# Gate/up products of the FFN by seven block products in place of eight, and SwiGLU values split at the down projection

## The chip, the core and the metric

The kernel runs on one core of one Trainium2 chip. The metric is the device time of one execution in microseconds (us), as the median of several executions. The engines are TensorE (PE, with its weight loads as PEld), VectorE (DVE), ScalarE (ACT), GpSimd (POOL) and SyncE (SP, which here only issues transfers). Each engine works through its own instructions in their order. A matmul sums into a bank of PSUM; VectorE and ScalarE read PSUM, GpSimd works on SBUF here.

## What is computed

One transformer block on 512 latent tokens and 256 context tokens of width 1024: adaLN, a token mixer of retention and latent attention, an output projection, and then the part that the change touches, two norms around a SwiGLU FFN with D_FF = 2816:

```python
def _swiglu(h, w_gu, w_down):
    a, b = jnp.split(h @ w_gu, 2, axis=-1)
    return (jax.nn.silu(a) * b) @ w_down
...
        x = _layer_norm(alpha * x + g1 * y_l, ln1_g[i], ln1_b[i])
        x = _layer_norm(alpha * x + g2 * _swiglu(x * (1.0 + s2) + sh2, w_gu[i], w_down[i]), ln2_g[i], ln2_b[i])
```

All operands are float32. `w_gu` is 1024 x 5632: `a` (gate) and `b` (up) have 2816 columns each, that is 22 column tiles of 128.

## The kernel before

**Pairs.** [...] `split` (L104) makes a pair: ScalarE copies the operand with rounding to H (L105), VectorE subtracts H from it and has L (L106). `mm3` multiplies two pairs by three matmuls, HH (L121), HL (L122) and LH (L123). `weight` loads 512 KB of a weight from SyncE's queue and splits it.

**Stages around the change.** The tokens are two halves (`tp`) of 256. The output projection ends with a half's `first_norm`, which makes the normalised rows `z` and then, in `to_features`, transposes them on TensorE (L863), applies the modulation and splits the result to `h2`, the moving operand of gate/up: 8 k-blocks of 128 features by 512 tokens. While the second half is normalised, the first half of NEARLY = 2 early column tiles runs (matmuls of 256 columns, weights `wgh`, `wgl`); their second half follows.

Then come the other 20 column tiles, one after the other. Each has two weights, gate and up, and for each of them 8 k-blocks x 3 matmuls of 512 columns into a bank `gu` of its own: 48 matmuls. `activate` reads both banks: ScalarE's silu of the gate (L916), VectorE's multiply with the up product (L917), and a split into the pair `tt` for the down projection (L105, L106).

The down projection has 22 weights. Its first pass (`pair_mm`) does the first two tiles of 128 tokens with each weight, 12 matmuls of 512 columns; the second pass does the other two, with the last norm of the first ones beside it, and ends in `last_norm`, whose additions on POOL (L1019) are among the last operations. The rows `z` of the first norm stay in SBUF as `x1`; they are scaled by `ln1_g` and `ln1_b` in the middle of the gate/up stage and used as the residual.

**What sets the order.** The code is written in the order wanted, and a tile layer turns it into one instruction stream per engine, with semaphores for what must wait. Buffers come from pools: three raw weights, three pairs of weights, pages of 4 KB per partition, 8 buffers `e8` and 6 `hp`, two PSUM buffers of two banks (`big`) and four of one bank (`bank`). A tile can be written again when all that read it are done; this is kept per tile, not per part of it.

## Time and profile before

| | |
|---|---|
| median of 3 runs | 1004.62 us (1004.43 to 1005.13) |
| span of the profiled execution | 1001.1 us |
| time of the median around that span | 3.5 us |
| instructions in the trace | 11924 |
| TensorE busy | 97% of the span, 4652 matmuls |
| VectorE, ScalarE, GpSimd busy | 62%, 40%, 4% |

The profile is of one execution. The span runs from its first to its last instruction. The device time has some microseconds around it; here the median of the runs is 3.5 us above this span. "L123" is line 123 of the kernel; matmuls are pipelined, so one begins while the one before it is still shown as busy.

### The profile page before, as it was taken

What the parts mean: (1) busy time and instruction counts of PE and PEld (TensorE: products, weight loads), DVE (VectorE), ACT (ScalarE), POOL (GpSimd) and SP (SyncE); (2) the same over time, 40 slices, a digit from 0 to 9 for tenths busy, and PEclk for the clock granted to TensorE, in tenths of its full rate; (3) what the DMA queues carried; (4) which work ended last, traced back from release to release, by engine and by line L of the source; (5) the groups of instructions that cost most, each with busy time, mean ns of one, the idle gap of its engine ahead of it and who ended that gap; (6) DMA issues with size and microseconds to landing.
All of it is one profiled execution on the core that took longest, in us unless ns stands there. A gap on an engine that the chain in (4) does not pass through costs nothing.

```text
span 1001.1 us, 11924 instructions
## 1 busy us (share of the span) xinstructions
PE 971.0 (97%) x4652; PEld 790.0 (79%) x4652; DVE 616.5 (62%) x945; ACT 400.2 (40%) x596; POOL 42.2 (4%) x77
## 2 busy tenths in 40 slices
...
GB/s 356 317 137 200 238 78 44 22 64 48 28 96 156 136 211 255 152 79 22 0 1 64 150 206 150 84 84 90 100 126 105 87 102 89 148 208 190 213 229 60
DMA packets 40360, 128.22 MB, mean 128 GB/s; under 512 B 6768, under 2 KB 7920, under 8 KB 40304
## 3 DMA queue, kind: packets, MB, share of 16 engines
...
q0 software_dynamic: 640, 1.57, 0.8%
q8 instruction: 36, 0.59, 0.2%
q14 instruction: 20, 0.16, 0.1%
...
## 4 chain that ended last, share of the span: by engine, by line
PE 90%; DVE 5%; DMA 2%; ACT 1%; POOL 1%; issue 1%; POOLq 0%; SPq 0%; DVEq 0%; ACTq 0%
PE gu L122 8%; PE gu L123 8%; PE gu L121 8%; PE wd L122 4%; PE wd L121 4%; PE wd L123 4%; PE gt L121 3%; PE gt L123 3%; PE gt L122 3%; PE rva L121 1%; PE rva L123 1%; PE rva L122 1%; PE st L121 1%; PE av L121 1%; PE po L654 1%; PE po L656 1%
## 5 line engine op out<-in xcount | busy, mean ns | idle before, releaser
L106 DVE TENSOR_TENSOR w<-wr,w 128x1024 fp32r<-128x1024 f32 (+2 forms) x158 | 190.0, 1204 | 186.1 <-ACT w L105 185.7
L105 ACT CAST w<-wr 128x1024 fp32r<-128x1024 f32 (+2 forms) x158 | 163.1, 1033 | 268.3 <-issue 78.8
L123 PE MATMUL gu<-h,w 128*128 128x512 f32 x320 | 126.6, 396 | 0.0
L122 PE MATMUL gu<-h,w 128*128 128x512 f32 x320 | 126.5, 395 | 0.0
L121 PE MATMUL gu<-h,w 128*128 128x512 f32 x320 | 125.9, 393 | 0.0
L122 PEld LDWEIGHTS gu<-h,w 128*128 128x128 f32 x320 | 60.2, 188 | 14.6
L121 PEld LDWEIGHTS gu<-h,w 128*128 128x128 f32 x320 | 60.0, 188 | 14.4
L123 PEld LDWEIGHTS gu<-h,w 128*128 128x128 f32 x320 | 60.1, 188 | 13.7
L122 PE MATMUL wd<-w,tt 128*128 128x512 f32 (+1 forms) x163 | 61.0, 374 | 0.0
L123 PE MATMUL wd<-w,tt 128*128 128x512 f32 (+1 forms) x163 | 60.9, 374 | 0.0
L121 PE MATMUL wd<-w,tt 128*128 128x512 f32 (+1 forms) x163 | 60.7, 373 | 0.0
L121 PE MATMUL gt<-hL,w 128*128 128x512 f32 x128 | 50.9, 398 | 0.2 <-DVE ck L484 0.2
L122 PE MATMUL gt<-hL,w 128*128 128x512 f32 x128 | 50.7, 396 | 0.0
L123 PE MATMUL gt<-hL,w 128*128 128x512 f32 x128 | 50.7, 396 | 0.0
L917 DVE TENSOR_TENSOR sa<-gu,sa 128x512 f32<-128x512 f32 (+1 forms) x24 | 15.5, 646 | 56.9 <-PE gu L123 55.7
L916 ACT ACTIVATE sa<-gu 128x512 f32<-128x512 f32 (+1 forms) x24 | 13.5, 564 | 83.4 <-PE gu L123 83.4
L149 DVE SCALAR_TENSOR_TENSOR junk<-wr,sc 128x1024 bf16<-128x1024 f32 x20 | 24.5, 1223 | 26.6 <-DMA wr<-in_wada_dram 25.9
L121 PEld LDWEIGHTS wd<-w,tt 128*128 128x128 f32 x163 | 30.6, 188 | 6.1
L123 PEld LDWEIGHTS wd<-w,tt 128*128 128x128 f32 x163 | 30.7, 188 | 6.0
L122 PEld LDWEIGHTS wd<-w,tt 128*128 128x128 f32 x163 | 30.6, 188 | 6.0
L405 POOL TENSOR_SCALAR sm<-sm 128x1 f32<-128x1 f32 x18 | 7.8, 436 | 639.0 <-DVE sm L825 562.6
L106 DVE TENSOR_TENSOR pt<-ex,pt 128x512 fp32r<-128x512 f32 x48 | 30.7, 686 | 4.0 <-ACT pt L105 4.0
...
## 6 DMA issues: line engine op xcount, KB each, us to landing
wr<-in_w_gu_dram SPq DMA_DIRECT2D x44, 512.0 KB, 3.5
wr<-in_w_dn_dram SPq DMA_DIRECT2D x44, 512.0 KB, 3.5
wr<-in_wada_dram SPq DMA_DIRECT2D x20, 512.0 KB, 4.1
wr<-in_w_out_dram SPq DMA_DIRECT2D x16, 512.0 KB, 3.4
ada_m<-in_wada_dram SPq DMA_DIRECT2D x12, 512.0 KB, 6.2
ada_s<-in_wada_dram SPq DMA_DIRECT2D x8, 512.0 KB, 8.9
ada_h<-in_wada_dram SPq DMA_DIRECT2D x8, 512.0 KB, 8.9
wr<-in_w_rg_dram SPq DMA_DIRECT2D x8, 512.0 KB, 8.9
```

The lines of the kernel that those rows point to most:

```text
L105: S.copy(h, src)
L106: V.tensor_tensor(l, src, h.bitcast(F32), ALU.subtract)
L121: T.matmul(o, st[0], mv[0], start=start, stop=False)
L122: T.matmul(o, st[0], mv[1], start=False, stop=False)
L123: T.matmul(o, st[1], mv[0], start=False, stop=stop)
L149: V.scalar_tensor_tensor(junk, raw, 1.0, vec, ALU.mult, ALU.mult, accum_out=acc[:, b:b + 1])
L405: G.tensor_scalar(dst, src, scale, eps, ALU.mult, ALU.add)
L654: T.matmul(po[:65], vh, pt[:, 0], start=j == 0, stop=False)
L656: T.matmul(po[:65], vh, pt[:, 1], start=False, stop=j == NTA - 1)
L916: S.activation(sa, pab[0], AF.Silu)
L917: V.tensor_tensor(sa, pab[1], sa, ALU.mult)
```

## The change

A column tile's gate and up weights together are a matrix of 1024 x 256, seen as 2 x 2 blocks of 512 x 128: A11, A12 are the gate's two halves of k, A21, A22 the up's. The moving operand is 2 x 2 blocks of 512 features by 256 tokens: B11, B12 the first 512 features of the two halves of tokens, B21, B22 the other 512. The change forms the product of the blocks by the seven products of Winograd's form of Strassen's scheme, for 20 tiles. The first two tiles keep eight.

- Weights: S1 = A21 + A22, S2 = S1 - A11 on VectorE (L986, L987), S3 = A11 - A21, S4 = A12 - S2 on POOL (L988, L989), each 128 x 512 per tile, and then six pairs per two tiles in place of four: the gate's whole weight, S1 with S2, S3 with S4 (128 x 1024 each), and A22 (128 x 512).
- Moving operand, once: T1 = B12 - B11, T2 = B22 - T1 on VectorE, T3 = B22 - B12, T4 = B21 - T2 on POOL, each 128 x 1024 and split.
- Products, each 4 k-blocks x 3 matmuls of 256 columns: P1 = A11 B11, P2 = A12 B21, P3 = S4 B22, P4 = A22 T4, P5 = S1 T1, P6 = S2 T2, P7 = S3 T3. A tile has 84 such matmuls. The sums of products are in part made in PSUM: P6, P7 and P4 accumulate on P1 in the bank `gy`, P3 on P5 in `gz`; P2 has a bank `gx`. Between them ScalarE copies the sum after P1 (L1016), P6 (L1026) and P5, and VectorE reads it after P2 (L1021), P7 (L1035), P3 (L1039) and P4 (L1044).
- Tiles come in ten pairs; each product runs for both tiles of a pair in turn, and the two `gy` banks are one tile of the pool (`big("gy")`). The weights' loads, sums and splits of the next pair are written between the products.
- The SwiGLU values stay float32 in pages `tv`, and `hidden` splits them at the down projection, one tile per weight of the first pass.
- `to_features` makes the features of four k-blocks in one page `hx` and splits them in twos (`hb`); the rows `z` go to DRAM (`zkeep`), from ScalarE's queue, and come back (`kept`) in the first pass of the down projection.

The diff, cut to its core:

```diff
+    def pair_pages(src, n):
+        a, b = page([P, 4, 256], F32R, n + "h"), page([P, 4, 256], F32R, n + "l")
+        for j in range(0, 4, 2):
+            split(a[:, j:j + 2], b[:, j:j + 2], src[:, j:j + 2])
+        return a, b
     def to_features(tp, zs):
-        c = slice(tp * 256, tp * 256 + 256)
         for g in range(2):
             ps = big("zt")
             for f in range(4):
                 for i in range(2):
                     T.transpose(ps[:, f // 2, (f % 2) * 256 + i * P:(f % 2) * 256 + (i + 1) * P],
                                 zs[i][:, (4 * g + f) * P:(4 * g + f + 1) * P], ident)
-            for f in range(4 * g, 4 * g + 4):
-                src = ps[:, f % 4 // 2, (f % 2) * 256:(f % 2 + 1) * 256]
-                S.activation(h2[f][:, 0, c], src, AF.Identity, bias=sh2[:, f:f + 1], scale=sc2[:, f:f + 1])
-                hf = half([P, 256], n="hf")
-                if f % 2 == 0:
-                    V.tensor_scalar(hf, src, sc2[:, f:f + 1], sh2[:, f:f + 1], ALU.mult, ALU.add)
+            hf = hx[g, tp] = page([P, 4, 256], n="hx")
+            for j in (0, 2, 1, 3):
+                f = 4 * g + j
+                src = ps[:, j // 2, (j % 2) * 256:(j % 2 + 1) * 256]
+                if j < 2:
+                    V.tensor_scalar(hf[:, j], src, sc2[:, f:f + 1], sh2[:, f:f + 1], ALU.mult, ALU.add)
                 else:
-                    S.activation(hf, src, AF.Identity, bias=sh2[:, f:f + 1], scale=sc2[:, f:f + 1])
-                V.tensor_tensor(h2[f][:, 1, c], hf, h2[f][:, 0, c].bitcast(F32), ALU.subtract)
+                    S.activation(hf[:, j], src, AF.Identity, bias=sh2[:, f:f + 1], scale=sc2[:, f:f + 1])
+            hb[g, tp] = pair_pages(hf, "hb")
             yield
...
+            nc.scalar.dma_start(zkeep[2 * tp + i], z)
...
-                feat_mm(ps[:, :256], wg[2 * f + s], lambda k: (h2[k][:, 0, c], h2[k][:, 1, c]))
+                feat_mm(ps[:, :256], wg[2 * f + s], lambda k: (hb[k // 4, tp][0][:, k % 4], hb[k // 4, tp][1][:, k % 4]))
                 pab.append(ps[:, :256])
-            activate(pab, tt[f], c, 256)
-    x1 = zs[0] + zs[1]
-    for f in range(NEARLY, FT):
-        pab = []
-        for s in range(2):
-            w = weight(w_gu[2 * f + s])
-            ps = bank("gu")
-            feat_mm(ps, feat(w), lambda k: (h2[k][:, 0], h2[k][:, 1]))
-            pab.append(ps)
-        t = (eight if f < 8 else page)([P, 2, NL], F32R, "tt")
-        activate(pab, t, slice(0, NL), NL)
-        tt.append(t)
-        if f == 9:
-            l1g = rowb(lnrow[0])
-            l1b = rowb(lnrow[1])
-        if 9 <= f < 13:
-            V.tensor_tensor(x1[f - 9], x1[f - 9], l1g, ALU.mult)
-            V.tensor_tensor(x1[f - 9], x1[f - 9], l1b, ALU.add)
+            sa = half([P, 256], n="sa")
+            S.activation(sa, pab[0], AF.Silu)
+            V.tensor_tensor(tv[0][:, f, c], pab[1], sa, ALU.mult)
+    def moving(src, n):
+        a, b = eight([P, 4, 256], F32R, n + "h"), eight([P, 4, 256], F32R, n + "l")
+        split(a, b, src)
+        return a, b
+    def difference(a, b, n, eng):
+        t = page([P, 4, 256], n=n)
+        eng.tensor_tensor(t, a, b, ALU.subtract)
+        return t
+    t1 = difference(hx[0, 1], hx[0, 0], "t1", V)
+    t2 = difference(hx[1, 1], t1, "t2", V)
+    T2 = moving(t2, "t2")
+    T1 = moving(t1, "t1")
+    t3 = difference(hx[1, 1], hx[0, 1], "t3", G)
+    T3 = moving(t3, "t3")
+    t4 = difference(hx[1, 0], t2, "t4", G)
+    T4 = moving(t4, "t4")
+    B11, B21, B22 = hb[0, 0], hb[1, 0], hb[1, 1]
+    def product(o, st, mv, more=False):
+        for k in range(4):
+            c = slice(k * P, (k + 1) * P)
+            mm3(o, (st[0][:, c], st[1][:, c]), (mv[0][:, k], mv[1][:, k]), k == 0 and not more, k == 3, more)
+    class Hidden:
+        def __init__(self, f):
+            self.f = f
+        def loads(self):
+            self.a = load(w_gu[2 * self.f], 1024)
+            self.b = page([P, 1024], n="wgb")
+            nc.sync.dma_start(self.b, w_gu[2 * self.f + 1])
+        def sums(self):
+            ga, gb = self.a, self.b
+            s = self.s12 = page([P, 2, 512], n="s12")
+            d = self.s34 = page([P, 2, 512], n="s34")
+            V.tensor_tensor(s[:, 0], gb[:, :512], gb[:, 512:], ALU.add)
+            V.tensor_tensor(s[:, 1], s[:, 0], ga[:, :512], ALU.subtract)
+            G.tensor_tensor(d[:, 0], ga[:, :512], gb[:, :512], ALU.subtract)
+            G.tensor_tensor(d[:, 1], ga[:, 512:], s[:, 1], ALU.subtract)
+        def split_a(self):
+            w = whl.tile([P, 2, 1024], F32R, tag="w", name=nm("w"))
+            split(w[:, 0], w[:, 1], self.a)
+            self.a11, self.a12 = [(w[:, 0, c], w[:, 1, c]) for c in (slice(0, 512), slice(512, 1024))]
+        def halves(self, s, n):
+            a, b = page([P, 2, 512], F32R, n + "h"), page([P, 2, 512], F32R, n + "l")
+            split(a, b, s)
+            return [(a[:, i], b[:, i]) for i in range(2)]
+        def split_12(self):
+            self.s1, self.s2 = self.halves(self.s12, "s12")
+        def split_34(self):
+            self.s3, self.s4 = self.halves(self.s34, "s34")
+        def split_22(self):
+            w = page([P, 2, 512], F32R, "a22")
+            split(w[:, 0], w[:, 1], self.b[:, 512:])
+            self.a22 = w[:, 0], w[:, 1]
+        def p1(self):
+            self.o = tv[self.f // 2][:, self.f % 2]
+            self.qz = half([P, 2, 256], n="qz")
+            product(self.y, self.a11, B11)
+            S.copy(self.qz[:, 0], self.y)
+        def p2(self):
+            x = bank("gx")[:, :256]
+            product(x, self.a12, B21)
+            V.tensor_tensor(self.o[:, :256], x, self.qz[:, 0], ALU.add)
+        def p6(self):
+            self.ub = half([P, 2, 256], n="ub")
+            product(self.y, self.s2, T2, True)
+            S.copy(self.ub[:, 0], self.y)
+        def p5(self):
+            self.z = bank("gz")[:, :256]
+            product(self.z, self.s1, T1)
+            S.copy(self.qz[:, 1], self.z)
+        def p7(self):
+            product(self.y, self.s3, T3, True)
+            V.tensor_tensor(self.ub[:, 1], self.y, self.qz[:, 1], ALU.add)
+        def p3(self):
+            product(self.z, self.s4, B22, True)
+            V.tensor_tensor(self.o[:, 256:], self.z, self.ub[:, 0], ALU.add)
+            S.activation(self.o, self.o, AF.Silu)
+        def p4(self):
+            product(self.y, self.a22, T4, True)
+            V.tensor_tensor(self.o[:, :256], self.y, self.o[:, :256], ALU.mult)
+            V.tensor_tensor(self.o[:, 256:], self.ub[:, 1], self.o[:, 256:], ALU.mult)
+    def steps(h, names):
+        if h is not None:
+            for n in names.split():
+                getattr(h, n)()
+    hid = {f: Hidden(f) for f in range(NEARLY, FT)}
+    steps(hid[NEARLY], "loads sums split_a split_12 split_34")
+    steps(hid[NEARLY + 1], "loads sums split_a split_12 split_34 split_22")
+    steps(hid[NEARLY], "split_22")
+    steps(hid.get(NEARLY + 2), "loads")
+    for f in range(NEARLY, FT, 2):
+        tv.append(page([P, 2, NL], n="tv"))
+        y = big("gy")
+        both = [hid[f + i] for i in range(2)]
+        for i in range(2):
+            both[i].y = y[:, i, :256]
+        c, d, e = hid.get(f + 2), hid.get(f + 3), hid.get(f + 4)
+        for what, ahead in (("p1", [(d, "loads"), (c, "sums split_a")]), ("p2", [(c, "split_12")]),
+                            ("p6", [(c, "split_34")]), ("p5", [(e, "loads"), (c, "split_22"), (d, "sums split_a")]),
+                            ("p7", [(d, "split_12")]), ("p3", [(d, "split_34")]), ("p4", [(d, "split_22")])):
+            for h in both:
+                steps(h, what)
+            for h, n in ahead:
+                steps(h, n)
...
+    def kept(t):
+        z = page([P, 1024], n="x1")
+        nc.scalar.dma_start(z, zkeep[t])
+        V.tensor_tensor(z, z, l1g, ALU.mult)
+        V.tensor_tensor(z, z, l1b, ALU.add)
+        x1.append(z)
+    tt = []
+    def hidden():
+        k = len(tt)
+        if k < FT:
+            t = (eight if 3 <= k < 11 else page)([P, 2, NL], F32R, "tt")
+            split(t[:, 0], t[:, 1], tv[k // 2][:, k % 2])
+            tt.append(t)
...
+    for _ in range(3):
+        hidden()
     acc = accumulators(0, "wd")
     for k in range(FT):
         w = weight(w_dn[k])
+        hidden()
         pair_mm(acc, (w[:, 0], w[:, 1]), tt, k, FT, 0)
+        if k in (8, 11, 14, 17):
+            kept(len(x1))
```

What this does to the order of the instructions shows in three places. The first is PE inside the stage. Before, the 24 matmuls of a weight follow each other, and the first of the next weight waits for its cast only (`h` the features, `w` the weight, the row's last figures the shape):

```order
L123 MATMUL gu958_5628<-h2848_4857,w957_5625 128x512
L121 MATMUL gu958_5628<-h2849_4858,w957_5625 128x512
L122 MATMUL gu958_5628<-h2849_4858,w957_5625 128x512
L123 MATMUL gu958_5628<-h2849_4858,w957_5625 128x512
L121 MATMUL gu963_5664<-h2842_4851,w962_5661 128x512 [waits Activation_49]
```

After, at the seventh pair, where P1 of its first tile ends and P1 of its second begins (`gy1147` is the pair's double bank, `gx` that of P2):

```order
L122 MATMUL gy1147_7036<-hbl892_5139,w1124_6831 128x256
L123 MATMUL gy1147_7036<-hbh891_5138,w1124_6831 128x256
L121 MATMUL gx1155_7078<-hbh897_5163,w1124_6831 128x256
L122 MATMUL gx1155_7078<-hbl898_5164,w1124_6831 128x256
L123 MATMUL gx1155_7078<-hbh897_5163,w1124_6831 128x256
L121 MATMUL gx1155_7078<-hbh897_5163,w1124_6831 128x256
L121 MATMUL gy1147_7036<-hbh891_5138,w1140_6939 128x256 [waits Activation_49]
```

Four matmuls of P2 have been put between the two P1, and the second P1 waits for ScalarE, which copies the first one's sum out of the same tile `gy1147`.

The second is VectorE in the stage. Before, it alternates weight splits (L106) with the multiply and the split of `activate`:

```order
L106 TENSOR_TENSOR w957_5625<-wr956_5623,w957_5625 128x1024 [waits DMAHW1_49,PE_49,Activation_49]
L917 TENSOR_TENSOR sa952_5588<-gu950_5562,sa952_5588 128x512 [waits PE_49]
L106 TENSOR_TENSOR w962_5661<-wr961_5659,w962_5661 128x1024 [waits DMAHW2_49,Activation_49]
L106 TENSOR_TENSOR tt951_5587<-sa952_5588,tt951_5587 128x512 [waits Activation_49]
L106 TENSOR_TENSOR w965_5691<-wr964_5689,w965_5691 128x1024 [waits DMAHW3_49,PE_49,Activation_49]
L917 TENSOR_TENSOR sa960_5654<-gu958_5628,sa960_5654 128x512 [waits PE_49]
```

After, at the end of a pair (`s34l` and `a22` belong to the next pair's weights, L1039 is the sum after P3, L1044 and L1045 the multiplies after P4):

```order
L1039 TENSOR_TENSOR tv1116_6791<-gz1133_6898,ub1129_6866 128x256 [waits PE_49]
L106 TENSOR_TENSOR s34l1144_7001<-s341139_6934,s34h1143_7000 128x1024 [waits DVE_49,Activation_49]
L1039 TENSOR_TENSOR tv1116_6791<-gz1134_6912,ub1130_6880 128x256 [waits PE_49]
L1044 TENSOR_TENSOR tv1116_6791<-gy1117_6792,tv1116_6791 128x256 [waits PE_49,Activation_49]
L1045 TENSOR_TENSOR tv1116_6791<-ub1129_6866,tv1116_6791 128x256 [waits DVE_49]
L106 TENSOR_TENSOR a221145_7032<-wgb1121_6823,a221145_7032 128x512
L1045 TENSOR_TENSOR tv1116_6791<-ub1130_6880,tv1116_6791 128x256 [waits Activation_49]
L986 TENSOR_TENSOR s121152_7069<-wgb1136_6928 128x512 [waits DMAHW0_49]
L1044 TENSOR_TENSOR tv1116_6791<-gy1117_6792,tv1116_6791 128x256 [waits PE_49]
```

The multiplies after P4 now stand among the splits and sums of the next pair's weights: the read of `gy` (L1044) follows the split of 128 x 1024.

The third is ScalarE at the start of the stage. Before, the silus of the early tiles' second half and the casts of the first whole tiles' weights and values:

```order
L916 ACTIVATE sa941_5467<-gu939_5417 128x256 [waits PE_49]
L105 CAST tt911_5225<-sa941_5467 128x256 [waits DVE_49]
L916 ACTIVATE sa944_5522<-gu942_5472 128x256 [waits PE_49,Activation_49]
L105 CAST tt912_5226<-sa944_5522 128x256 [waits DVE_49]
L916 ACTIVATE sa952_5588<-gu947_5532 128x512 [waits PE_49]
L105 CAST w957_5625<-wr956_5623 128x1024 [waits DMAHW1_49]
L105 CAST w962_5661<-wr961_5659 128x1024 [waits DMAHW2_49,PE_49]
```

After (`t1h` to `t4h` are the moving sums' casts, `qz` the copies after P1, `ub` those after P6, `s12h` and `s34h` weight sums):

```order
L940 ACTIVATE sa928_5439<-gu926_5389 128x256 [waits PE_49]
L105 CAST t2h934_5499<-t2933_5497 128x1024 [waits DVE_49]
L105 CAST t1h936_5503<-t1932_5495 128x1024
L940 ACTIVATE sa931_5492<-gu929_5442 128x256 [waits PE_49]
L105 CAST t3h939_5509<-t3938_5507 128x1024 [waits Pool_49]
L105 CAST t4h942_5515<-t4941_5513 128x1024 [waits Pool_49]
L1016 COPY qz968_5573<-gy967_5572 128x256 [waits PE_49]
L1016 COPY qz969_5587<-gy967_5572 128x256 [waits PE_49]
L105 CAST s12h949_5532<-s12946_5523 128x1024 [waits DMAHW4_49,DVE_49]
L105 CAST s34h951_5536<-s34947_5524 128x1024 [waits Pool_49]
L1026 COPY ub979_5646<-gy967_5572 128x256 [waits PE_49]
```

The four casts of the moving sums, two of which wait for POOL, have come ahead of the copies after P1 and the casts of the weight sums.

## Rows read from the trace of the kernel before

**Rows 1.** Part 1 of the page: engines' busy us (share of span) xinstructions.

```profile
PE 971.0 (97%) x4652; PEld 790.0 (79%) x4652; DVE 616.5 (62%) x945; ACT 400.2 (40%) x596; POOL 42.2 (4%) x77
```

**Rows 2.** Part 4 of the page: engines' shares of the chain that ended last.

```profile
PE 90%; DVE 5%; DMA 2%; ACT 1%; POOL 1%; issue 1%; POOLq 0%; SPq 0%; DVEq 0%; ACTq 0%
```

**Rows 3.** The windows view, the steady stretch of the gate/up stage; first its columns.

```profile
core 0: us, PE busy (x) PEld busy (x) DVE busy (x) ACT busy (x) POOL busy (x), PEclk, DMA share, GB/s
646.00:869.00 223.00, 223.00 (x960) 180.24 (x959) 82.21 (x87) 60.98 (x79) 0.00 (x0) 1.00 0.29 97
```

**Rows 4.** Groups by line, PE: xcount | busy us, mean ns | idle.

```profile
L123 PE MATMUL gu<-h,w 128*128 128x512 f32 x320 | 126.6, 396 | 0.0
```

**Rows 5.** Timeline of PE (start us, us): first matmuls of two stages.

```profile
645.81 0.39 PE L121 MATMUL gu<-h,w 128*128 128x512 f32 x1
...
869.03 0.40 PE L121 MATMUL wd<-w,tt 128*128 128x512 f32 x1
```

**Rows 6.** The timeline of PE: the early tiles' first half, second and last matmul.

```profile
619.33 0.28 PE L122 MATMUL gu<-h,wgh 128*128 128x256 f32 x1
...
630.41 0.28 PE L123 MATMUL gu<-h,wgl 128*128 128x256 f32 x1
```

**Rows 7.** The timeline of DVE in two places where it works without a pause.

```profile
575.00 0.69 DVE L800 TENSOR_TENSOR mt<-mt,gate 128x512 f32<-128x512 f32 x1
575.60 1.22 DVE L106 TENSOR_TENSOR w<-wr,w 128x1024 fp32r<-128x1024 f32 x1
576.74 0.69 DVE L106 TENSOR_TENSOR mg<-mt,mg 128x512 fp32r<-128x512 f32 x1
...
627.21 0.42 DVE L917 TENSOR_TENSOR sa<-gu,sa 128x256 f32<-128x256 f32 x1
627.55 0.68 DVE L824 BATCH_NORM_STATS2 st<-z 128x6 f32<-128x512 f32 x1
```

**Rows 8.** Groups of ACT by line and shape, as the stage uses.

```profile
L105 ACT CAST w<-wr 128x1024 fp32r<-128x1024 f32 x150 | 157.1, 1048 | 256.0 <-issue 78.8 <-PE wd L123 54.8 <-DVE junk L149 25.7
L105 ACT CAST tt<-sa 128x512 fp32r<-128x512 f32 x20 | 12.3, 615 | 0.0
L916 ACT ACTIVATE sa<-gu 128x256 f32<-128x256 f32 x4 | 1.5, 383 | 3.4 <-PE gu L123 3.4
```

**Rows 9.** Timeline at the end: POOL's two 128x512 operations and DVE's.

```profile
988.74 0.68 DVE L1003 SCALAR_TENSOR_TENSOR z<-z,z 128x512 f32<-128x512 f32 x1
988.78 1.79 POOL L1019 TENSOR_TENSOR z<-z,row 128x512 f32<-128x512 f32 x1 [0.84 <-ACT z L1018]
...
995.97 0.75 DVE L1016 SCALAR_TENSOR_TENSOR z<-z,sm,row 128x512 f32<-128x512 f32 x1 [0.43 <-POOL sm L406]
996.76 1.26 POOL L1019 TENSOR_TENSOR z<-z,row 128x512 f32<-128x512 f32 x1 [0.83 <-ACT z L1018]
```

**Rows 10.** The page's part 6: the gate/up weights' DMA, xcount, KB, us to landing.

```profile
wr<-in_w_gu_dram SPq DMA_DIRECT2D x44, 512.0 KB, 3.5
```

**Rows 11.** The timeline where a product of an early tile ends and is read.

```profile
641.32 0.28 PE L123 MATMUL gu<-h,wgl 128*128 128x256 f32 x1
...
641.64 0.39 ACT L916 ACTIVATE sa<-gu 128x256 f32<-128x256 f32 x1 [1.24 <-PE gu L123]
```

**Rows 12.** The timeline where TensorE waits for a VectorE result.

```profile
631.94 0.44 PE L863 MATMUL zt<-ident,z 128*128 128x128 f32 x2 [1.13 <-DVE z L887]
```

**Rows 13.** The windows view, ten us of the second first norm's features.

```profile
630.00:640.00 10.00, 8.37 (x69) 7.91 (x69) 7.85 (x16) 5.80 (x13) 0.95 (x2) 1.00 0.35 113
```

**Rows 14.** The windows view, ten us of the down projection.

```profile
920.00:930.00 10.00, 10.00 (x45) 8.09 (x44) 4.69 (x4) 3.71 (x4) 0.00 (x0) 1.00 0.66 197
```

**Rows 15.** The timeline of PE behind its longest wait in the retention's output.

```profile
392.02 0.50 PE L121 MATMUL ro<-gtd,w 128*128 128x512 f32 x1 [3.01 <-ACT w L105]
```

**Rows 16.** The windows view, the same place.

```profile
394.00:398.00 4.00, 4.00 (x13) 3.10 (x12) 2.34 (x5) 1.05 (x1) 0.00 (x0) 0.57 0.80 232
398.00:402.00 4.00, 4.00 (x19) 3.24 (x18) 2.93 (x5) 1.05 (x1) 0.00 (x0) 1.00 0.84 266
```

26 lines of the change are left out of this document (12 added, 14 removed).

## The prediction

> **What bounds the kernel now.** I read the page's engine shares first: TensorE is busy 971.0 of 1001.1 us, VectorE 616.5, ScalarE 400.2, GpSimd 42.2 [rows 1]. The chain that ended last says the same: 90% of it is TensorE [rows 2]. Then the stage itself. From 646 to 869 us TensorE has 960 matmuls and is busy all 223 us at full granted clock, while VectorE works 82 us, ScalarE 61 us and GpSimd not at all [rows 3]. So this stage has one limit, the matmul stream, and slack on three engines. Work taken from TensorE is worth its full time as long as the others, who get more to do, don't make TensorE wait.
>
> The length of a matmul in the trace is no measure of that stream, because matmuls overlap: a 512-column one shows 396 ns [rows 4]. What counts is the distance between starts. The 960 of 512 columns start from 645.81, and the first matmul of the down projection starts at 869.03 [rows 5]: 223.22 us, 232.5 ns each. The 256-column ones of the first half of the early tiles run from 619.33 to 630.41 with 94 steps in between [rows 6]: 117.9 ns each. Two halves (235.8) cost 1.4% more than one whole.
>
> **The change part by part.**
>
> *The matmuls.* Per column tile 48 matmuls of 512 columns become 7 x 4 x 3 = 84 of 256 columns; 20 tiles make 1680. 1680 x 117.9 ns = 198.1 us in place of 223.2: 25.1 us saved, if the stream never stops. The early two tiles, and the count of down-projection matmuls, are unchanged.
>
> *The other engines' throughput.* Two tiles form a pair, 168 matmuls, 19.8 us of TensorE. VectorE gets per pair: six splits of 1024 columns, six 512-wide operations (sums and A22's split), and ten of 256. Back to back these start 1.14, 0.60 and 0.34 us apart [rows 7]: 6.8 + 3.6 + 3.4 = 13.8 us. ScalarE: 6 x 1.05 + 4 x 0.62 + 6 x 0.38 = 11.1 us by durations [rows 8]. GpSimd: four differences of 128x512. The trace has two such operations, 1.79 and 1.26 us [rows 9]: 5.0 to 7.2 us. Each alone is below 19.8, so I charge nothing for throughput; if that cover went, the excess would be paid ten times. The weights arrive as before: 0.5 MB per 4.9 us instead of 5.6, against 3.5 us to landing [rows 10].
>
> *GpSimd beside VectorE.* The GpSimd operation of 1.79 us starts 0.04 behind a VectorE operation with two SBUF inputs, at 988.78, and ends at 990.57, that is 1.15 after the VectorE operation has ended (988.74 + 0.68 = 989.42); the one of 1.26 starts at 996.76, when VectorE has just ended (995.97 + 0.75), and runs alone [rows 9]. So the first reads as if it had stood still while VectorE ran. [...]
> Added up from rows, VectorE's operations with two SBUF inputs make 6.8 + 3.6 + 0.7 = 11.1 us per pair; with 2.7 us of operations that read PSUM and 5.0 to 7.2 us of GpSimd it is 18.8 to 21.0 against 19.8. I take the lower end, since the 0.53 between the two GpSimd operations is time that VectorE's own operation has in the sum already, and keep the upper one as a rival.
>
> *New waits on the way of TensorE.* This is the term I am least sure of. Three of a tile's products (P6, P7, P4) accumulate on the bank of P1, and between them the partial sum has to be read out. A wait for it is due four times per pair, and harder than the code shows: both tiles' sums lie in one double bank `gy`, and the program's order shows the second tile's product waiting for the read-out of the first's. Between stand fillers from other products, 3 to 15 matmuls, 4 at P1 in most pairs. What such a read-out takes, from rows: the group's last matmul starts at 641.32 and ends 0.28 later, ScalarE starts 0.04 after and runs 0.39 [rows 11]. With as much again for the way back to TensorE it is 0.75 us by ScalarE, and 0.78 by VectorE, whose 256-wide operation takes 0.42 [rows 7]. Four fillers and the step itself give 5 x 0.118 = 0.59: short by 0.16. Eleven, as at P7 and P4 of the pair shown, give 1.41: enough.
> That holds for an idle reader. Ahead of P6's copy on ScalarE stands a 1.05 us cast that becomes ready about when the copy should; ahead of P4's multiply on VectorE stand a 1.22 us split and two 256-wide operations. Lower bound per pair: 2 x 0.16 = 0.3. Upper bound, each read-out behind one whole long operation: 2 x (0.16 + 1.05) + 2 x (0.78 + 1.22 - 1.41) = 3.6. Walking the queues of the pair in the program's order, I get 0.2 at P1, 0.25 at P6, 0 at P7, 0.5 at P4 (its split waits for the long one before it), and 0.15 for weight loads that no matmul covers after a stop: **1.1 us per pair, 11 for ten pairs** (3 to 36).
>
> *Entry.* Between the early tiles and P6 of the first pair, T1 to T4 (the four sums of the moving operand) and two tiles' weight sums have to be made. On VectorE this is four splits, two differences and one weight sum before s12 is whole: 7 x 1.14 + 2 x 0.6 + two 256-wide multiplies 0.7, 9.9 us; on ScalarE the two casts that wait for GpSimd's T3 and T4 (two operations of twice 1.26) stand ahead of them. TensorE has in that time half of the early second half (48 matmuls) and P1 and P2 of both tiles (48): 11.3 us, from about when the last of the features arrives, and loses less than it seems. The features themselves come in a chain of waits as before (1.6 us idle in 630 to 640, at full clock [rows 13]). I count 0.8 us for features that come later, since a whole block is cast before the first product, 1.5 for the first s12 and 0.2 for the second: **2.5 us** (0 to 6; a gain is excluded, because before nothing is idle here after 641).
>
> *Exit.* The last P4 and the first down products share a bank and a multiply that stands behind a 1.22 us split, with four fillers: **0.7 us** (0 to 2). In the first pass of the down projection VectorE now has 1.14 + 0.60 us and ScalarE 1.05 + 0.62 per weight of 12 x 0.2325 = 2.79 us; the 22 moved splits, and the reload of four rows of tokens with two 1.22 us operations each, fit beside 100% TensorE, where VectorE now works 4.7 of 10 us [rows 14]. I price them at nothing; without that cover it would be 22 x 0.60 = 13 us. The writes of those rows go out from ScalarE's queue, ahead of the features there; their issue is part of the 0.8 above.
>
> Sum: 198.1 + 11 + 2.5 + 0.7 = 212.3 us for what takes 223.2. The span becomes 1001.1 - 10.9 = 990.2, and with the 3.5 us by which the median 1004.62 stands above this execution's span, **993.7 us**.
>
> **The rivals.**
>
> *Full gain.* The waits are hidden and the entry is short: 198.1 + 3 + 0.5 + 0.2 = 201.8, so 983.2 us. For it: each engine has slack. Against: four fillers are shorter than the shortest read-out.
>
> [...] GpSimd at 1.79 us each makes the pair 21.0 us by sum, and the waits of 1.1 come on top: 22.1 x 10 + 3.2 = 224.2, 1005.6 us. For it: rows 9. Against: only two instances.
>
> *The read-outs are caught (slower than before).* If the four waits take more than (223.2 - 198.1 - 3.2) / 10 = 2.19 us per pair, the kernel gets slower; at the upper bound of 3.6 it is 237.3 for 223.2, 1018.7 us. For it: in-order queues with operations of 1.05 and 1.22 us, 56 and 70% full. Against: the fillers, and that the long ones mostly have their inputs earlier.
>
> [...]
> [...]
>
> **How the numbers follow.** The forecast, a partial gain that ends between 988 and 1001: 0.54. Full gain: 0.16. Shared port: 0.13. Caught read-outs: 0.12. Clock: 0.05. A difference of 0.2%, 2 us, is about what a measurement of this kernel can tell from no change. Faster by more than that are the first two and a small part of the port's case, the one in which the waits are shorter than I took them (0.03): 0.73. Within it falls most of the port's case: 0.08. Slower are its rest (0.02), the caught read-outs and the clock: 0.19. For eight in ten the range takes in the full gain, with a little below it because the entry may cost nothing, and the port's case up to its price of 1005.6: 982 to 1005.6.
>
> **What would show it.** Matmuls of 256 columns 118 ns apart in the stage; idle of TensorE of some 1 us per pair in lines of `gy`, released by lines 1016, 1026 (ScalarE) and 1035, 1044 (VectorE); GpSimd differences near 1.3 us. Wrong would be: a pair longer than 22 us, a granted clock below 1.00 in the stage, GpSimd operations near 1.8 us or longer with VectorE waiting beside them, or idle before the down projection's weights in its first pass.

## The result, and the profile after

The changed kernel takes 1016.19 us (median, 1015.32 to 1017.55) where the kernel before takes 1004.58: a ratio of 1.0115, interval 1.0100 to 1.0129. It is slower by 1.2%; the forecast was 993.7, and the range ended at 1005.6. Its profiled execution has a span of 1013.9 us.

Parts 1 and 4 of its page, against [rows 1, 2]:

```profile
PE 960.7 (95%) x5372; PEld 813.6 (80%) x5372; DVE 727.5 (72%) x1101; ACT 453.2 (45%) x690; POOL 104.7 (10%) x119
...
PE 74%; DVE 13%; DMA 5%; ACT 3%; issue 2%; POOL 1%; POOLq 0%; ACTq 0%; SPq 0%; DVEq 0%
```

TensorE's share of the chain falls from 90% to 74%, and VectorE's rises from 5% to 13%: TensorE now waits for others inside the stage that had one limit before [rows 3]. The windows view shows where; the first line is the columns, the second most of the stage, the others three stretches at its entry:

```profile
core 0: us, PE busy (x) PEld busy (x) DVE busy (x) ACT busy (x) POOL busy (x), PEclk, DMA share, GB/s
705.00:855.00 150.00, 142.88 (x1154) 137.59 (x1153) 111.85 (x150) 72.11 (x112) 37.64 (x28) 1.00 0.32 99
620.00:630.00 10.00, 6.20 (x40) 6.24 (x41) 8.53 (x15) 3.78 (x6) 0.73 (x2) 0.83 0.19 55
660.00:670.00 10.00, 7.66 (x48) 7.17 (x48) 6.17 (x5) 3.70 (x6) 2.52 (x3) 0.83 0.32 105
670.00:680.00 10.00, 8.40 (x57) 8.20 (x58) 7.20 (x8) 4.99 (x8) 2.48 (x2) 0.83 0.45 157
```

At 0.118 us each, 150 us have room for 1271 matmuls; 1154 are there, although the clock is 1.00. At the entry TensorE is idle for up to 3.8 of 10 us, and the granted clock falls to 0.83.

The part of the kernel ahead of the change varies: the output projection's first matmul starts anywhere between 570.3 and 575.3 us in the profiles of this study. So I count from that matmul. From there to the end before took 1001.1 - 571.2 = 429.9 us, after 1013.9 - 571.6 = 442.3: 12.4 more. It divides like this:

| stretch | before | after | difference |
|---|---|---|---|
| first output-projection matmul to first early gate/up matmul | 47.9 | 52.2 | +4.3 |
| from there to the first down-projection matmul | 249.9 | 256.7 | +6.8 |
| of it, fewer and shorter matmuls (25.1 us, and 12 of the last P4 that now stand behind the first down-projection matmul) | | | -26.6 |
| of it, entry: to the start of the third pair (77.7 us for 492 matmuls of 0.1179, and 4.1 of idle and transposes as before) | | | +15.6 |
| of it, pairs 3 to 10: 179.0 us for 1368 matmuls | | | +17.7 |
| down projection to the end (with those 12 matmuls, 1.4 us) | 132.1 | 133.4 | +1.3 |

A pair has 168 matmuls, but 36 of the second pair run behind the third pair's first one, so they are counted where they ran. So the saving is there in full, and 37 us of waits came with it. What TensorE waits for, by engine and line (total us, times, longest), leaving out the waits ahead of the change:

```profile
...
PE gy L121 <- DVE tv L1044: 6.0, 6, 1.6
PE gu L121 <- DVE z L833: 4.6, 1, 4.6
PE gy L121 <- DVE ub L1035: 4.5, 5, 1.8
PE gy L121 <- ACT s12h L105: 3.6, 2, 1.9
...
PE gy L123 <- DVE s12l L106: 2.4, 3, 1.3
PE gy L121 <- ACT hx L880: 1.5, 1, 1.5
PE gu L122 <- DVE hbl L106: 1.5, 1, 1.5
```

In the pairs it is VectorE's reads of `gy` (L1035, L1044) that come late; none of the waits listed there ends with a copy of ScalarE's. From the third pair on the two make 9.1 us. The rest of the 17.7 lies in steps that the list leaves out, because a matmul is shown as busy for 0.28 us where the next could start after 0.118: the part of a wait that this covers, a late second matmul behind most stops (0.1 us each), and 12 steps in which ScalarE's copies (L1016, L1026) end last, 2.0 us together. Why VectorE is late shows in its timeline at the end of the fourth pair (start, us):

```profile
748.61 0.41 DVE L1039 TENSOR_TENSOR tv<-gz,ub 128x256 f32<-128x256 f32 x1
...
748.85 1.30 POOL L988 TENSOR_TENSOR s<-wr,wgb 128x512 f32<-128x512 f32 x1 [2.90 <-PE gz L122]
748.94 1.76 DVE L106 TENSOR_TENSOR a<-wgb,a 128x512 fp32r<-128x512 f32 x1
...
750.62 0.68 DVE L986 TENSOR_TENSOR s<-wgb 128x512 f32<-128x512 f32 x1
751.22 0.41 DVE L1039 TENSOR_TENSOR tv<-gz,ub 128x256 f32<-128x256 f32 x1
...
752.49 0.41 DVE L1044 TENSOR_TENSOR tv<-gy,tv 128x256 f32<-128x256 f32 x1
752.64 1.29 POOL L989 TENSOR_TENSOR s<-wr,s 128x512 f32<-128x512 f32 x1 [2.49 <-DVE s L987]
752.82 1.39 DVE L1045 TENSOR_TENSOR tv<-ub,tv 128x256 f32<-128x256 f32 x1
...
752.95 0.39 PE L121 MATMUL gy<-t4h,a 128*128 128x256 f32 x1 [1.60 <-DVE tv L1044]
```

The split of A22 takes 1.76 us in place of 0.68: it starts 0.09 after a GpSimd difference, and ends 0.55 after it. All that is queued behind it moves by a microsecond, the read L1044 among it, and TensorE stands for 1.60 us. The second difference stretches a 0.41 us multiply (L1045) to 1.39 in the same way. The groups say it of the whole stage (count | busy us, mean ns):

```profile
L106 DVE TENSOR_TENSOR s12l<-s,s12h 128x1024 fp32r<-128x1024 f32 x20 | 28.0, 1402 | 11.9 <-ACT s12h L105 9.5 <-PE gz L122 1.6 <-ACT qz L1031 0.7
L106 DVE TENSOR_TENSOR a<-wgb,a 128x512 fp32r<-128x512 f32 x20 | 18.0, 904 | 0.0
L1045 DVE TENSOR_TENSOR tv<-ub,tv 128x256 f32<-128x256 f32 x20 | 11.6, 597 | 0.0
L1044 DVE TENSOR_TENSOR tv<-gy,tv 128x256 f32<-128x256 f32 x20 | 8.3, 415 | 2.2 <-PE gy L123 2.2
L988 POOL TENSOR_TENSOR s<-wr,wgb 128x512 f32<-128x512 f32 x20 | 32.9, 1643 | 98.0 <-DVE a L106 37.0 <-PE gz L123 28.7 <-DVE s34l L106 10.5
L989 POOL TENSOR_TENSOR s<-wr,s 128x512 f32<-128x512 f32 x20 | 25.9, 1293 | 50.1 <-DVE s L987 50.1
```

Operations of VectorE with two SBUF inputs (splits, sums, L1045) are stretched; one that reads PSUM (L1044) keeps its 0.415, also in the seven cases in which a GpSimd operation ran beside it (0.41 to 0.43). In 640 to 880 us, 45 operations with two SBUF inputs overlap a GpSimd operation. All 34 that start behind it are longer than the shortest of their kind, by 0.06 to 1.78 us, 26.9 us together; 3.1 of that are two splits beside T3 and T4, which e1 and e3 below still have. The 11 that start ahead of it are not longer (0.02 us at most), and there it is GpSimd that waits: its difference takes 1.3 to 1.8 us, and 1.27 at the shortest. Of the 31 operations that read PSUM beside one, none is longer (0.40 to 0.43 us).

### The profile page after: what moved, and what is told of

Same layout as the page of the kernel before. It is cut to its first block, busy times and chain, and to the rows that moved or that the text cites. A ratio compares the mean times of both kernels' runs of the same rounds, so it can differ in the third digit from the quotient of the medians.

```text
span 1013.9 us, 13755 instructions
## 1 busy us (share of the span) xinstructions
PE 960.7 (95%) x5372; PEld 813.6 (80%) x5372; DVE 727.5 (72%) x1101; ACT 453.2 (45%) x690; POOL 104.7 (10%) x119
## 4 chain that ended last, share of the span: by engine, by line
PE 74%; DVE 13%; DMA 5%; ACT 3%; issue 2%; POOL 1%; POOLq 0%; ACTq 0%; SPq 0%; DVEq 0%
PE wd L122 4%; PE wd L123 4%; PE wd L121 4%; PE gt L121 3%; PE gt L123 3%; PE gt L122 3%; PE gy L121 3%; PE gy L123 2%; DVE w L106 2%; PE gy L122 2%; DMA wr<-in_w_ro_dram 2%; PE rva L123 1%; PE rva L122 1%; PE rva L121 1%; DMA wr<-in_w_qk_dram 1%
## 5 line engine op out<-in xcount | busy, mean ns | idle before, releaser
L106 DVE TENSOR_TENSOR w<-wr,w 128x1024 fp32r<-128x1024 f32 (+2 forms) x138 | 169.4, 1228 | 96.6 <-ACT w L105 96.5
L105 ACT CAST w<-wr 128x1024 fp32r<-128x1024 f32 (+2 forms) x138 | 142.4, 1033 | 192.8 <-PE wd L123 51.0
L988 POOL TENSOR_TENSOR s<-wr,wgb 128x512 f32<-128x512 f32 x20 | 32.9, 1643 | 98.0 <-DVE a L106 37.0
L106 DVE TENSOR_TENSOR s12l<-s,s12h 128x1024 fp32r<-128x1024 f32 x20 | 28.0, 1402 | 11.9 <-ACT s12h L105 9.5
L105 ACT CAST s12h<-s 128x1024 fp32r<-128x1024 f32 x20 | 21.0, 1048 | 29.0 <-DVE s L987 28.0
L106 DVE TENSOR_TENSOR pt<-ex,pt 128x512 fp32r<-128x512 f32 x48 | 30.6, 684 | 4.1 <-ACT pt L105 4.0
L511 ACT ACTIVATE gate<-gt 128x512 f32<-128x512 f32 x16 | 9.6, 599 | 48.8 <-PE gt L123 48.8
L614 DVE TENSOR_REDUCE sm<-sc 128x1 f32<-128x768 f32 x32 | 29.6, 952 | 2.4 <-PE sc L613 2.0
L989 POOL TENSOR_TENSOR s<-wr,s 128x512 f32<-128x512 f32 x20 | 25.9, 1293 | 50.1 <-DVE s L987 50.1
L121 PE MATMUL gy<-t4h,a 128*128 128x256 f32 x80 | 23.8, 297 | 7.4 <-DVE tv L1044 6.0
L121 PEld LDWEIGHTS gt<-hL,w 128*128 128x128 f32 x128 | 24.1, 188 | 5.9 <-DVE ck L484 0.5
```

Of the source, the lines that this page charges most:

```text
L105: S.copy(h, src)
L106: V.tensor_tensor(l, src, h.bitcast(F32), ALU.subtract)
L121: T.matmul(o, st[0], mv[0], start=start, stop=False, skip_group_check=more)
L511: S.activation(dst[n // 2][:, n % 2], ps, AF.Sigmoid)
L614: V.tensor_reduce(mx[:, t:t + 1], ps.rearrange("p a b -> p (a b)")[:, :NA], AX.X, ALU.max)
L988: G.tensor_tensor(d[:, 0], ga[:, :512], gb[:, :512], ALU.subtract)
```

## The experiments

Theory **port** (a name; what the two engines share, no run shows): a GpSimd difference stops VectorE's two-input operations, and what is queued behind them on VectorE comes late for TensorE. Rival **bank**: both tiles' sums lie in one double bank, so each second product waits for a read whatever VectorE does. For the entry, rivals of its own follow below. Each ratio is to the kernel before on the same chip; "span" is counted from the first output-projection matmul (before 429.9), "matmuls" is their number in 705 to 855 us (room for 1271).

| kernel | ratio (95%) | span | first early matmul | matmuls |
|---|---|---|---|---|
| changed kernel | 1.0115 (1.0100 to 1.0129) | 442.3 | 52.2 | 1154 |
| e1 differences on VectorE | 0.9951 (0.9934 to 0.9967) | 425.2 | 51.7 | 1237 |
| e2 own banks | 1.0100 (1.0085 to 1.0116) | 438.1 | 52.4 | 1169 |
| e3 both | 0.9919 (0.9904 to 0.9933) | 421.4 | 51.5 | 1268 |
| e4 no differences | 0.9942 (0.9927 to 0.9956) | 422.9 | 52.2 | 1224 |
| e6 = e1 and unread differences | 1.0187 (1.0155 to 1.0219) | 446.5 | 51.4 | 1130 |
| e8 differences in quarters | 1.0214 (1.0183 to 1.0246) | 450.1 | 51.6 | 1105 |
| e5 = before and stores | 0.9999 (0.9985 to 1.0012) | 431.5 | 48.2 | |
| e7 = e3, rows stay | 0.9914 (0.9888 to 0.9939) | 420.2 | 49.1 | 1253 |
| e9 = e3, half blocks | 0.9924 (0.9912 to 0.9937) | 421.4 | 52.0 | 1268 |
| e10 = e9, T3, T4 on VectorE | 0.9916 (0.9903 to 0.9930) | 421.4 | 52.3 | 1268 |
| e11 = e10, rows stay | 0.9915 (0.9902 to 0.9928) | 421.7 | 49.2 | 1252 |
| e12 = e3, start one pair later | 0.9950 (0.9937 to 0.9962) | 423.9 | 51.6 | 1265 |
| e13 = e12, T3, T4 on VectorE | 0.9951 (0.9939 to 0.9963) | 424.2 | 52.1 | 1268 |
| e14 = e3, two rows stay | 0.9908 (0.9894 to 0.9922) | 418.6 | 49.3 | 1263 |
| e15 = e3 again | 0.9927 (0.9913 to 0.9941) | 421.8 | 51.8 | 1268 |

### e1, e2, e3: port and bank, one by one and together

```diff
-            G.tensor_tensor(d[:, 0], ga[:, :512], gb[:, :512], ALU.subtract)
-            G.tensor_tensor(d[:, 1], ga[:, 512:], s[:, 1], ALU.subtract)
+            V.tensor_tensor(d[:, 0], ga[:, :512], gb[:, :512], ALU.subtract)
+            V.tensor_tensor(d[:, 1], ga[:, 512:], s[:, 1], ALU.subtract)
```

> Edit: the weight differences S3 and S4 of lines 988 and 989 go from GpSimd to VectorE, nothing else. The changed kernel is 1016.2 us. Port theory (a GpSimd difference holds up VectorE's operations with two SBUF inputs, so the reads of gy come late): VectorE is spared about 2.2 us of being held per pair of tiles and gets 4 x 0.60 = 2.4 us of work, so its total stays, but the 0.68 us operations no longer stretch to 1.4 us and more, and S3, S4 are ready earlier; 1006 to 1014 us. Shared-bank theory (both tiles' sums in one double bank make the second tile wait for the first's read, whatever VectorE does): 1014 to 1018 us.

```diff
-        y = big("gy")
         both = [hid[f + i] for i in range(2)]
         for i in range(2):
-            both[i].y = y[:, i, :256]
+            both[i].y = big("gy")[:, 0, :256]
```

> Edit: each tile of a pair gets a gy buffer of its own, so that the second tile's product no longer waits for the read of the first tile's sum. Shared-bank theory: the waits of TensorE in lines of gy for L1035 and L1044 (4.5 and 6.0 us) and the small steps of 0.15 to 0.3 us at P1 and P6 (some 4 us) go, 1001 to 1006 us. Port theory: VectorE is as late as before, and TensorE waits for the splits of the weight sums or for the same reads one product later; 1010 to 1017 us.

> Both edits: the differences on VectorE and a gy buffer per tile. If the two causes are separate and both count: 996 to 1003 us. If the shared bank alone counts: as the kernel with own buffers, within 2 us. If the port alone counts: as the kernel with the differences on VectorE, within 2 us. What stays above 198.1 us for 1680 products is then the entry (about 16 us above the work from the first early matmul to the third pair).

Moving four operations of 0.68 us per pair **to** the busier engine is worth 17 us of span; the bank alone 4. Even the port theory had expected less of e1. The edit of e2 has a second effect: a pair now holds both buffers, so the first P1 of the next pair waits for the last read of this one. The waits for L1035 fall from 4.5 to 1.7 us, but those for L1044 grow:

```profile
PE gy L121 <- DVE tv L1044: 10.4, 8, 2.4
```

The same late reads are met one product further on, at that P1. With both edits the pairs run without a gap:

```profile
705.00:855.00 150.00, 150.00 (x1268) 149.56 (x1268) 118.17 (x186) 77.68 (x122) 0.00 (x0) 1.00 0.36 116
```

1268 matmuls in 150 us are 118.3 ns each, the distance of [rows 6], with VectorE at 79% and ScalarE at 52%. From the start of the fourth pair to the first down matmul a pair takes 21.8 us in the changed kernel (152.4 for seven), 20.8 in e2, 20.4 in e1 (20.6 less 0.2, since 12 matmuls more run in that stretch) and 19.9 in e3: against e3 the differences on GpSimd alone cost 0.9, the double bank alone 0.5 and both 1.9. The third pair of the changed kernel, with VectorE still behind from the entry, takes 26.6 and makes the mean of the eight 22.4.

### e4, e6: is it the operation or its lateness?

```diff
-            G.tensor_tensor(d[:, 0], ga[:, :512], gb[:, :512], ALU.subtract)
-            G.tensor_tensor(d[:, 1], ga[:, 512:], s[:, 1], ALU.subtract)
...
-            self.s3, self.s4 = self.halves(self.s34, "s34")
+            self.s3, self.s4 = self.halves(self.s12, "s34")
```

> Edit: the two GpSimd differences per tile are left out, and the S1/S2 sums are split a second time in their place, so the output is not the reference's; casts, splits, matmuls and reads keep their number and size. Port theory: in the pairs from the third on, the 20.5 us above the pure matmul time fall to 6 to 10 us, since no GpSimd operation runs there; 1003 to 1008 us. Shared-bank theory: those 20.5 us stay, 1014 to 1017 us.

The pairs from the third on then take 166.5 us for 1356 matmuls, 6.7 above the pure time, in the range that the port theory gave (6 to 10), and little different from e1 (4.9); the entry gained too, so the total fell below the 1003 us it gave. e6 turns the question round: VectorE makes the differences that are used, and GpSimd makes them once more for nobody.

```diff
+            G.tensor_tensor(spare, ga[:, :512], gb[:, :512], ALU.subtract)
+            G.tensor_tensor(spare, ga[:, 512:], s[:, 1], ALU.subtract)
```

> Edit: the differences are on VectorE, as in the kernel of ratio 0.995, and GpSimd makes them too, into a buffer that nobody reads. Port theory (VectorE's operations with two SBUF inputs stand still while a GpSimd operation runs): the results of GpSimd matter to nobody, but the time goes back to that of the changed kernel or above, since VectorE has the work and the stops: ratio 1.010 to 1.020. Rival (the GpSimd results came late, 1.3 to 1.7 us each with the wait for them): ratio 0.994 to 0.997, as without them.

From 0.9951 to 1.0187, by results that nothing waits for. TensorE's longest sum of waits in the stage of e6 (its lines from the splits on are numbered 4 higher, so L1039 is the read after P7, L1035 elsewhere) and the stretched split, in e6 and then in e1:

```profile
PE gy L121 <- DVE ub L1039: 11.0, 11, 2.4
```

```profile
L106 DVE TENSOR_TENSOR s12l<-s,s12h 128x1024 fp32r<-128x1024 f32 x20 | 32.2, 1608 | 5.4 <-ACT s12h L105 2.9 <-PE gz L122 1.6 <-ACT qz L1035 0.7
...
L106 DVE TENSOR_TENSOR s12l<-s,s12h 128x1024 fp32r<-128x1024 f32 x20 | 24.3, 1216 | 6.0 <-ACT s12h L105 3.5 <-PE gz L122 1.6 <-ACT qz L1031 0.7
```

The split takes 1608 ns, 1216 in e1. The lateness of GpSimd's results is not the cause; its running beside VectorE is. (The order of the instructions is made anew for each kernel, so not each of the 21 us is proved to come from GpSimd's running beside VectorE. A raw weight is also held until GpSimd has read it, but from 640 to 885 us TensorE and VectorE never wait for a load in e6, and ScalarE does for 0.3 us.)

### e8: shorter GpSimd instructions

```diff
-            G.tensor_tensor(d[:, 0], ga[:, :512], gb[:, :512], ALU.subtract)
+            for q in range(4):
+                c = slice(q * P, q * P + P)
+                G.tensor_tensor(d[:, 0, c], ga[:, c], gb[:, c], ALU.subtract)
...
```

> Edit: the changed kernel with each GpSimd difference of 512 columns made in four instructions of 128 columns. If VectorE is held for one whole GpSimd instruction at a time, it now stands still for about 0.3 to 0.4 us at a time in place of up to 1.6: ratio 1.000 to 1.008. If it is held for as long as GpSimd has work queued: 1.010 to 1.015. If the small instructions cost GpSimd much more time than the large ones and VectorE is held as often: above 1.015.

VectorE is indeed held less, by 14.0 us in 640 to 880 in place of 26.9. But a quarter costs GpSimd nearly half of the whole in the mean, so a difference takes 2.5 to 3.2 us. The shortest quarter takes 0.45 us, the shortest whole 1.27; the longer ones wait for an operation of VectorE that started ahead of them. (Lines here are numbered anew too: L990 and L993 are the two differences.)

```profile
L990 POOL TENSOR_TENSOR s<-wr,wgb 128x128 f32<-128x128 f32 x80 | 61.5, 799 | 87.9 <-issue 34.7 <-PE gz L123 23.8 <-PE gy L123 12.7
L993 POOL TENSOR_TENSOR s<-wr,s 128x128 f32<-128x128 f32 x80 | 47.8, 627 | 18.3 <-DVE s L987 18.3
```

```profile
ACT s34h L105 <- POOL s L993: 24.7, 11, 2.8
```

Now it is the lateness: ScalarE's cast of S3 and S4 waits 24.7 us for GpSimd (2.2 in the changed kernel), and VectorE's split behind it. The third branch of the expectation.

### e5, e7, e14: the entry, stores of z

In the changed kernel the load of the first gate/up weight behind the four of the early tiles is issued at 613.54, and ScalarE's cast of it, which stands ahead of the features' second block, waits for it; the early matmuls then start 4.6 us after TensorE was ready. What ends that wait is VectorE's read of the output projection's sum (L833), which frees a bank of PSUM and stands behind those features' splits in VectorE's queue:

```profile
613.54 0.33 SPq L110 DMA_DIRECT2D wr<-in_w_gu_dram  x1
...
617.86 1.05 ACT L105 CAST w<-wr 128x1024 fp32r<-128x1024 f32 x1 [2.26 <-DMA wr<-in_w_gu_dram]
...
623.80 0.35 PE L121 MATMUL gu<-hbh,wgh 128*128 128x256 f32 x1 [4.59 <-DVE z L833]
```

```diff
             zs.append(z)
+            nc.scalar.dma_start(zkeep[2 * tp + i], z)
```

> Edit: the kernel before, with one thing of the change added: ScalarE's queue writes each normalised row block z (four of 512 KB) to DRAM, nothing reads it. Store theory (the writes take the DMA engines while the output projection's last weights and the first gate/up weight come in, so the features of the first half come late): the first early matmul starts 3 to 5 us later, ratio to the kernel before 1.003 to 1.006. Rival (the late start comes from features made and split in whole blocks): ratio 0.999 to 1.001.

```diff
-            nc.scalar.dma_start(zkeep[2 * tp + i], z)
+            zrows.append(z)
...
-        z = page([P, 1024], n="x1")
-        nc.scalar.dma_start(z, zkeep[t])
+        z = zrows[t]
```

> Edit: on the kernel with the differences on VectorE and own gy buffers (ratio 0.9919): the rows z are not written to DRAM and fetched again, they stay in their pages until the second norm. Store theory: the wait of 4.7 us before the first early matmul goes to below 1.5 us, ratio 0.986 to 0.988. Rival (features in whole blocks are what is late): the wait stays, ratio 0.991 to 0.993. Third: four pages fewer for weights and sums make TensorE wait in the pairs: above 0.993.

In e14 this holds for the first half's two rows only, and e15 is e3 once more, beside it.

> Edit: on the kernel with the differences on VectorE and own gy buffers (ratio 0.9919): the rows z of the first half of the tokens stay in SBUF, those of the second half are written to DRAM as before, when fewer loads are under way. Store theory (the first half's writes delay the loads of the last output weights and of the first gate/up weight, whose cast stands ahead of the features on ScalarE): the wait of 4.7 us before the first early matmul falls to 1.5 us and the stretch of low clock behind it (2.0 us) goes, as where all rows stay, but with two pages taken in place of four the pairs keep 19.8 us; 4 to 5 us less than the kernel it starts from, ratio 0.986 to 0.988. Rival (two pages are too many as well): pairs of 20 to 23 us, ratio 0.990 to 0.993.

> The kernel with the differences on VectorE and own gy buffers once more, beside the one before on the same chip: ratio 0.9904 to 0.9933, pairs of 19.7 to 20.4 us from the fourth on, a wait of 4.5 to 5 us before the first early matmul.

The stores alone do nothing to the kernel before (first early matmul 48.2 against 47.9), though the same load is issued 2.4 us later with them (613.58 for 611.23): ScalarE comes to its cast at 617.84, behind most of the features, and does not wait for it. Without the stores, e7 starts the early matmuls 2.4 us sooner than e3, the wait is 1.5, and the clock stays up where e3 falls to 0.68 (window 620 to 630 us of e7, then of e3):

```profile
620.00:630.00 10.00, 8.51 (x71) 8.27 (x70) 9.67 (x17) 2.76 (x4) 0.87 (x3) 1.00 0.35 107
...
620.00:630.00 10.00, 8.28 (x52) 8.31 (x53) 9.10 (x15) 2.88 (x4) 0.73 (x2) 0.68 0.38 119
```

In the total it is hardly seen: span 420.2 for 421.4, since the pairs then do 1253 matmuls in the place of 1268. With two rows kept (e14) they do 1263, and the span is 418.6, the shortest of all; its ratio, 0.9908, overlaps with that of e15, 0.9927, on the same chip. So by the spans of single executions the first half's stores cost some 3 us, in the changed order only; the ratios do not tell this from nothing.

### e9, e10, e11: features in half blocks, T3 and T4 on VectorE

```diff
-            hf = hx[g, tp] = page([P, 4, 256], n="hx")
+            hf = hx[g, tp] = [page([P, 2, 256], n="hx") for _ in range(2)]
...
-    t3 = difference(hx[1, 1], hx[0, 1], "t3", G)
+    t3, _ = difference(hx[1, 1], hx[0, 1], "t3", V)
```

> Edit: on the kernel with the differences on VectorE and own gy buffers (ratio 0.9919), whose first early matmul starts 51.4 us after the first of the output projection (47.9 before): the features hx of a block of four are made in two buffers, VectorE's two and ScalarE's two, where one buffer held all four, so that the two engines no longer wait for each other in turn and a cast waits for its own two only. Whole-block theory (the entry is late because four features and their casts are one chain): the first early matmul comes 2 to 4 us earlier, and the second half's features too (the 1.5 us waits for hx and hbl halve); ratio 0.986 to 0.990. Rival (the stores of z and the loads behind them are what is late): ratio 0.991 to 0.993.

> Edit: as the kernel with two feature buffers, and T3 and T4 are made by VectorE too, so that GpSimd has no sums left. If GpSimd's two operations of 2.4 us hold VectorE at the entry (hbl, t2l stretched from 1.2 to 2.5 us): 2.5 us of holding go and 2.4 us of work come, T4's cast no longer waits for GpSimd, 1 to 2.5 us less than the kernel with two feature buffers. If TensorE does not wait for VectorE there: within 1 us of it.

> Edit: as the one before, and the rows z stay in SBUF in place of being written and fetched. Store theory: 1 to 3 us less than the one before, by an earlier first early matmul. If the pages are then short: TensorE waits for weights in the pairs, and it is slower than the one before by 1 us or more.

My theory of e9 fell: VectorE and ScalarE still take turns with the features, in buffers of their own (the wait for `hbl` halves, 1.47 to 0.72, and nothing follows from it). Why they take turns is open; the kernel before does it too. T3 and T4 on GpSimd stretch two splits at the entry of e3, one of 128x512 from 0.7 to 2.5 us and one of 128x1024 from 1.2 to 2.5. On VectorE (e10) they stretch none and the wait for `hbl` is gone, but other waits take its place, and the span stays 421.4. e11 is e7's finding again.

### e12, e13: a later start

```diff
+    for f in range(NEARLY, NEARLY + 2):
+        pab = []
+        for s in range(2):
+            w = weight(w_gu[2 * f + s])
+            ps = bank("gu")
+            for tp in range(2):
+                feat_mm(ps[:, tp * 256:tp * 256 + 256], feat(w), lambda k: (hb[k // 4, tp][0][:, k % 4], hb[k // 4, tp][1][:, k % 4]))
...
+    first = NEARLY + 2
```

> Edit: on the kernel with the differences on VectorE and own gy buffers (ratio 0.9919): the first pair of the scheme's tiles is computed by eight products (two tiles, 96 matmuls of 256 columns each, weights split as before), between the early tiles and the scheme, which then has nine pairs. It costs 2 x 12 x 0.118 = 2.8 us of matmuls. Entry theory (some 13 us between the first early matmul and the third pair are lost because the sums and splits of the moving operand and of two tiles' weights have to be made before P6, with nothing else for TensorE to do): 8 to 11 of them go, ratio 0.983 to 0.987. Rival (each start of the scheme costs that, wherever it stands, or the late features cost it): ratio 0.993 to 0.996.

> Edit: as the one before, and T3 and T4 are made by VectorE, so that GpSimd has no sums. If GpSimd's two operations of 2.4 us still hold VectorE where TensorE waits for it: 1 to 2.5 us less than the one before. With TensorE's work as cover: within 1 us of it.

Also missed. Between the first early and the first down matmul e12 has 238.5 us for 1896 matmuls (223.5): 15.0 above the work, e3 237.9 for 1872 (220.7): 17.2. The cover takes away 2 us and costs 2.8. What stays in e12: 4.4 us lost at the low clock (behind the late first matmul, behind the second half's features, behind the first pair's 2.1 us wait for L1035), and waits of 5.1 us. So a good part of the entry's cost is not a lack of cover. The waits that remain in e3, by size:

```profile
PE gu L121 <- DVE z L833: 4.7, 1, 4.7
PE gy L121 <- ACT s12h L105: 2.9, 2, 2.2
PE gy L121 <- DVE ub L1035: 2.5, 1, 2.5
...
PE gy L121 <- ACT hx L880: 1.5, 1, 1.5
PE gu L122 <- DVE hbl L106: 1.5, 1, 1.5
```

With some 3 us lost at the low clock these account for most of what e3 loses of the 25.1 us (it gains 429.9 - 421.4 = 8.5), also when the 2.5 us of waits that the kernel before has in this part are taken off. Which of them would go if features, sums and splits were put in another order was not tried.

## Why the prediction was wrong, point by point

**What bounds the kernel, and the matmuls.** Right: 118.3 ns per matmul of 256 columns where nothing is in the way (e3), and 25.1 us saved in TensorE's work.

**GpSimd beside VectorE.** This step failed. I had the row that shows it [rows 9], read it rightly as one engine standing still, and then priced it as a sum: 18.8 us of 19.8 per pair, so free. Two mistakes are in that. The stopping goes both ways: in [rows 9] GpSimd waited, in the stage it is more often VectorE that waits for the rest of a 1.3 us operation, 26.9 us in all. And what counts is not whether VectorE's queue is full but when its reads of `gy` come: they stand in order behind the stopped operation, and TensorE waits for them. e1 and e6 show it in both directions; in the whole span the step cost 17 us (442.3 for 425.2). In the changed kernel's trace, of 45 operations with two SBUF inputs beside a GpSimd one, the 34 that came second were stretched, by 26.9 us, and the 11 that came first were not; that the two engines share a port, as the name in the chances has it, no run shows. The price that I worked out from rows for that rival, 1005.6 us, counted GpSimd's 1.79 us as throughput and had no place for late reads.

**New waits.** Sized at 1.1 us per pair, measured 2.2 in the mean of pairs 3 to 10. The mechanism that I had walked through, short covers between read and next product in a shared double bank, is worth 0.5 where GpSimd is out of the way (e1 against e3), half of my figure. It was the rival "read-outs are caught" that came about (1018.7 us with 0.12, and it decides from 2.19 us per pair), but through VectorE's stopped operations and not through ScalarE's casts: L1016 and L1026 end none of the waits listed, only short steps of 2.0 us together.

**Entry.** This step failed too, and by more: sized at 2.5 us, measured 4.3 + 15.6 = 19.9. GpSimd's weight differences are the smaller part of it, since e1 without them still has 3.8 + 11.5 and e3 3.5 + 12.3. I had counted operations on VectorE and taken the matmuls of the early half as cover. In its place the trace shows a late first early matmul (4.3), waits up to the third pair that add up to 10.5 (hx 1.5, hbl 1.5, s12h 3.6, s12l 2.4, L1035 1.5), 4.0 us lost at the low clock in three stretches from 623.8, 662.7 and 672.7 us, each behind such a hole, and some 3 us of shorter steps; before had 4.1 us of idle and transposes in this place. Which order of features, sums and splits would have avoided the waits stays open, as no run here tried one. Of the writes of z I priced the issue; what they did was to the loads beside them: the cast that stands ahead of the features waits 2.26 us for its load in the changed kernel and 2.35 in e3, and not for the load in e7.

**The clock.** The chances gave a fall of the clock in the pairs 0.05. It did not come there: waits of up to 1.6 us left 705 to 855 at 1.00. At the entry it came three times, behind holes of 4.6, 1.7 and 1.9 us: 0.57 in 624 to 628, 0.50 in 662 to 664 and 0.52 in 672 to 674, with matmuls of 256 columns 0.213 us apart in place of 0.118. [rows 15, 16] show such a fall behind one wait, [rows 12, 13] none behind a shorter one, but the length of one hole does not decide: one of 1.79 us at 703.66 did nothing, nor did one of 2.5 in e3 (681.84); one of 1.66 at 660.95, with another of 0.5 us behind it, did. What decides it is not shown.

**Exit and moved splits.** From the first down matmul to the end e3 takes 132.1 us, as before: the 22 splits, the reloads and the stores cost nothing there, as priced. The changed kernel's 1.3 more is the 12 matmuls of the last P4 that stand behind the first down-projection matmul.

**Sum.** Pairs 17.7 (eight of them) for 11 (ten), entry 19.9 for 2.5, with the first two pairs in it, exit nothing for 0.7: 37 us of waits in place of 14.2. That e3 comes near the forecast (0.992; 993.7 us would be 0.989) does not bear the sum out: its pairs cost 0.8 for 11 and its entry 15.8 for 2.5, and the two errors nearly cancel. The range had 36 us as the pairs' worst case alone, but gave it 0.12; the entry's upper bound (6) was the one that was broken.
